# A decoder layer on one core: three seven-product pairs in the second half of the output linear, with sums of weights made beforehand

## The chip, the core and the metric

One Trainium2 core runs one decoder layer in float32. The metric is the time of one execution on the device, in microseconds (us); the median of several runs counts. The engines named here are TensorE (PE in the profile; PEld is its loading of weights), VectorE (DVE), ScalarE (ACT), GpSimd (POOL) and SyncE (SP). SP and POOL issue DMAs, each from a queue that it works off in order.

## What is computed

The layer takes 256 tokens and 16 learned tokens ahead of them (T = 272) of width 2048. It is a SwiGLU feed-forward block, then a mixer of differential attention and a short gated convolution, then a second SwiGLU block and a norm. Cut to what matters here, the reference is:

```python
s = s + 0.5 * swiglu_ffn(rms_norm(s, g1), w_gu1, w_down1)
h = rms_norm(s, g_mix)
q, k, v, b_gate, c_gate, u = jnp.split(h @ w_in, splits, axis=-1)
y_att, y_conv = diff_attention(q, k, v, ...), short_conv_mixer(b_gate, c_gate, u, conv_w)
z = einsum('blnw,nwd->blnd', stack([y_att, y_conv]), w_branch)
merged = sum(sigmoid(h @ w_gate) * z, axis=2)
s = s + merged @ w_out                # the output linear, 2048 x 2048
s = s + 0.5 * swiglu_ffn(rms_norm(s, g2), w_gu2, w_down2)
return rms_norm(s, g_final)[:, 16:]
```

## The kernel before, in words

**Precision.** Each float32 operand is split into a high part and a rest (`parts`, L551 and L552: ScalarE casts the high part, VectorE subtracts for the rest). A product of two blocks is three matmuls: high by high, low by high, high by low (L663 to L665 in `product`). A weight tile is 128 x 1024 (two blocks of 512 columns) or 128 x 512.

**Seven or eight products.** From the gates on, the linears run in `linear_mix`. It takes the 256 tokens as two halves and the columns as two halves of 512, and works through the depth in pairs of 128-row blocks. Each pair is a 2 x 2 by 2 x 2 block product and is one of three kinds:

- **D**: eight products, straight from the loaded weights (two tiles of 1024 columns).
- **S**: seven products in Strassen's manner. VectorE makes the sums of the weights from the loaded blocks just ahead of use (`sums`, L702 to L707), into two tiles t13 and t24.
- **P**: seven products, but t13 and t24 were made early in the kernel and stored in DRAM. The pair loads three blocks of weights (768 KB) and the two tiles (512 KB each, L692 and L693) where D and S load four blocks (1024 KB, L685).

S and P pairs split one tile of 512 columns and three of 1024. They also need sums of the activations: four blocks "sp" per pair, made by `sum_of_parts` on VectorE (L603 to L612), then ScalarE and VectorE (L634, L635). In the output linear those are kept in the pool `aux` (three buffers). A plan at the top of the file gives the kinds of the eight pairs, the positions at which results of an earlier linear are turned, and the tiles behind which `sums` of a later S pair is written. The output linear has two halves of 1024 output columns: `OUT_FIRST` ("DDSDSDSD", S in pairs 2, 4 and 6) and `OUT` ("DDDDSDSD"). `add_mix` (L1210) adds its products to the residual tiles sT. The down linears of the second feed-forward block run three times (thirds of its width) in the same way; the first half of the first two has the plan `DOWN_FIRST`.

**Order of the work.** The framework gives each engine its own order and buffers; the order in the trace is near that of the text but not the same. Weight loads are issued on SP: `load(p + 1)` is written behind the second tile of position p (`far` = 1 in the output linear, 2 in the gate-up linears that load P tiles into `aux`). Loaded weights have three buffers ("st"), split tiles four ("wh", "wl"), and the pool of sums "tt" two. Products are used at most three wide tiles behind their split (`step`, AHEAD = 3). After the last tile of a position one entry of the list `side` is run: transposes, sums and norms that belong to neighbours.

**Sums made early.** `Making` makes half a pair's t13 and t24: POOL fetches the four quarter blocks (L327), VectorE adds three times (L331 to L333), POOL stores (L339). `tick`, called once per 128 rows of the dense linears, spreads these makes over the first feed-forward block (512 ticks). `tick_later` spreads the list `MADE_LATER` over ticks 528 to 636, which are the linears v to u (attention runs beside them); there the makes use the two "tt" buffers. In order of time: first feed-forward block, q, b, then linears k, v, c and u (the ticks' stretch ends at tick 640 with u), gates and branch linears, the output linear's two halves, the second feed-forward block.

Of the kernel before, what the change touches and what calls it, by code (L numbers as in the profile page):

```python
# [9 lines left out]
F32 = mybir.dt.float32  # L10
F32R = mybir.dt.float32r
AF = mybir.ActivationFunctionType
ALU = mybir.AluOpType
# [36 lines left out]
FFN2 = ("DDPPDPPP", (1,), {}, ())  # L50
FFN2_MORE = ("DPPPDSPP", (2,), {(4, 1): 5}, ())
OUT_FIRST = ("DDSDSDSD", (1,), {(1, 1): 2, (3, 1): 4, (5, 1): 6}, ())
OUT = ("DDDDSDSD", (), {(3, 1): 4, (5, 1): 6}, ())
DOWN_FIRST = ("DDDDSDSD", (1,), {(3, 1): 4, (5, 1): 6}, ())
DOWN = ("DDSDSDSD", (), {(1, 1): 2, (3, 1): 4, (5, 1): 6}, ())
DOWN_LAST = ("DDDSDS", (1,), {(2, 1): 3, (4, 1): 5}, ())
# [13 lines left out]
GATE_UNITS = [GATES_FIRST] + [GATES] * (D // GW - 1)  # L70
MADE = [(0, d, p) for d, plan in enumerate(GATE_UNITS) for p, kind in enumerate(plan[0]) if kind == "P"]
MADE += [(1, u, p) for u in range(F // GW) for p, kind in enumerate(_unit_plan(u)[0]) if kind == "P"]
MADE_LATER = [(0, 0, 1), (0, 0, 3), (1, 1, 5), (1, 2, 1), (1, 3, 1)]
MADE = [m for m in MADE if m not in MADE_LATER]
LATER_TICKS = (TICK_COUNT + 16, TICK_COUNT + 124)

# [2 lines left out]
def decoder_layer(ctx: ExitStack, tc: tile.TileContext, t, out):  # L79
# [562 lines left out]
    def linear_mix(plan, a, w, name, done, k0=0, made=None, pairwise=False):  # L642

        kinds, turn_at, sums_at, by_load = plan
        nd = kinds.count("D")
        ns = len(kinds) - nd
        left = {k: 2 * nd * (k in "234x") + ns * (k != "x") for k in "1234567x"}
        ps = {}

        def product(k, left_op, wh, wl):
            first = k not in ps
            if first:
                ps[k] = bank(name + k)  # L660
            left[k] -= 1
            hi, lo = left_op
            nc.tensor.matmul(ps[k], hi, wh, start=first, stop=False)  # L663
            nc.tensor.matmul(ps[k], lo, wh, start=False, stop=False)  # L664
            nc.tensor.matmul(ps[k], hi, wl, start=False, stop=left[k] == 0)  # L665
            if left[k] == 0:
                done(k, ps[k])

        def use(p, n, products):

            for k, left_op, wh, wl in products:
                product(k, left_op, wh, wl)
            if p in turn_at and later:
                later.pop(0)()
            if n == (1 if kinds[p] == "D" else 3):
                if p == 0:
                    flush()
                if side:
                    side.pop(0)()

        def load(p):

            st = wpool.tile([P, 4, GW], F32, tag="st", bufs=ST_BUFS, name="st")
            n = 3 if p in by_load or kinds[p] == "P" else 4
            nc.sync.dma_start(out=st[:, :n, :], in_=w[k0 // 2 + p, :, :n, :])  # L685
            if kinds[p] == "P":
                if pairwise:
                    t13s[p] = wpool.tile([P, 2, GW], F32, tag="tt", bufs=2, name="t13")
                else:
                    t13s[p] = aux.tile([P, 2, GW], F32, tag="act", name="t13")  # L690
                t24s[p] = wpool.tile([P, 2, GW], F32, tag="tt", bufs=2, name="t24")
                nc.sync.dma_start(out=t24s[p], in_=made[p][:, 2:4, :])  # L692
                nc.sync.dma_start(out=t13s[p], in_=made[p][:, 0:2, :])  # L693
            if kinds[p] == "S":
                if not by_load and (made is None or pairwise):
                    t13s[p] = wpool.tile([P, 2, GW], F32, tag="tt", bufs=2, name="t13")
                elif p not in by_load:
                    t13s[p] = aux.tile([P, 2, GW], F32, tag="act", name="t13")
                t24s[p] = wpool.tile([P, 2, GW], F32, tag="tt", bufs=2, name="t24")
            return st  # L700

        def sums(k):  # L702
            st, t13, t24 = loaded[k], t13s[k], t24s[k]
            if k not in by_load:
                nc.vector.tensor_add(t13, st[:, 1:3, :], st[:, 3:4, :].to_broadcast([P, 2, GW]))
            nc.vector.tensor_add(t24[:, 0, :], t13[:, 0, :], st[:, 2, :])
            last_sum[:] = [nc.vector.tensor_add(t24[:, 1, :], t24[:, 0, :], st[:, 0, :]).ins]  # L707

        t13s, t24s = {}, {}

        def prefetch(p):
            t13 = t13s[p] = aux.tile([P, 2, GW], F32, tag="act", name="t13")
            nc.gpsimd.dma_start(out=t13, in_=w[k0 // 2 + p, :, 1:3, :])
            nc.gpsimd.dma_start(out=t13, in_=w[k0 // 2 + p, :, 3:5, :], accum_op=ALU.add)

        far = 2 if by_load or (made is not None and not pairwise) else 1
        loaded = {k: load(k) for k in range(far)}
        for p, kind in enumerate(kinds):
            for k in by_load:
                if k == p + 4 or (p == 0 and k < 4):  # L720
                    prefetch(k)
            st = loaded[p]
            (a11, a21), (a12, a22) = ([a.block(2 * p + c, i) for i in range(2)] for c in range(2))
            if kind == "D":
                tiles = [
                    (st[:, 1 - c :: 2, :], (("2", a1, 0), ("3", a1, 1), ("4", a2, 0), ("x", a2, 1)))
                    for c, (a1, a2) in enumerate(((a11, a21), (a12, a22)))
                ]
            else:
                s1, s2, s3, s4 = a.sums[p]  # L730
                tiles = [
                    (st[:, 2:3, :], (("3", s4, 0),)),
                    (st[:, 0:2, :], (("1", a11, 1), ("2", a12, 0))),
                    (t24s[p], (("6", s2, 0), ("4", a22, 1))),
                    (t13s[p], (("5", s1, 0), ("7", s3, 1))),
                ]
                if kind == "S" and p < len(kinds) - 1:
                    tiles[2:] = tiles[:1:-1]
            for n, (src, products) in enumerate(tiles):
                if n == 1 and p + far < len(kinds):  # L740
                    loaded[p + far] = load(p + far)
                wh, wl = parts(src, src.shape[1])
                if (p, n) in sums_at:

                    with tc.issue_after(part_last[1]):
                        sums(sums_at[p, n])
                products = [(k, left_op, wh[:, j, :], wl[:, j, :]) for k, left_op, j in products]
                step(lambda p=p, n=n, products=products: use(p, n, products), src.shape[1] > 1)
# [458 lines left out]
                out=lo, in0=src, scalar=gain, in1=hi.bitcast(F32), op0=ALU.mult, op1=ALU.subtract  # L1207
            )

    def add_mix(plan, a, w, k0, u, by, adds, end):  # L1210


        v = [[sT[i][u][:, q * GW : (q + 1) * GW] for q in range(2)] for i in range(2)]
# [45 lines left out]
            if all(n in ev for n in "1234567x"):  # L1259
                pending.append(finish_adds)  # L1260

        linear_mix(plan, a, w[u], "pd", done, k0)

    def out_done(u):
        def f():
            if u == 0:
                side.append(lambda: None)
                for p in (0, 2):
                    side.append(lambda p=p: [turned(p), turned(p + 1), squares(0, 0, p // 2), squares(1, 0, p // 2)])
                side.append(lambda: [hn.sum_of_parts(2, tmp), hn.sum_of_parts(3)])  # L1270
            else:
                side.extend(
                    (
                        lambda: [turned(4), squares(0, 1, 0), squares(1, 1, 0)],
                        lambda: [turned(5), hn.sum_of_parts(5)],
                        lambda: [turned(6), squares(0, 1, 1), hn.sum_of_parts(6)],
                        lambda: [turned(7), squares(1, 1, 1)],
                        lambda: hn.sum_of_parts(7),
                        norm_tok,
                    )  # L1280
                )

        return f
# [1 line left out]
    side.extend([lambda: None] * 2)  # L1285
    side.append(lambda: mo.sum_of_parts(6))
    add_mix(OUT_FIRST, mo, w_out, 0, 0, 1.0, "", out_done(0))
    add_mix(OUT, mo, w_out, 0, 1, 1.0, "", out_done(1))

    gfin = [apool.tile([P, W2], F32, tag="act", name=f"gfin{q}") for q in range(2)]  # L1290
    fss = const.tile([P, 2, 2 * 2 + 1], F32, name="fss")
# [32 lines left out]
    for half in thirds:  # L1324
# [14 lines left out]
        for u in range(2):  # L1339
# [32 lines left out]
            if final and u == 0:  # L1372
                side.append(lambda: None)
                side.extend(lambda p=p: ma.sum_of_parts(p) for p in (3, 5))
                add_mix(
                    DOWN_LAST, ma, w_down, half[0] * GC, u, 0.5, "side",
                    lambda score=score: side.extend(
                        lambda iq=iq: [score(*k) for k in iq] for iq in (((0, 0), (1, 0)), ((0, 1),), ((1, 1),))
                    ),
                )  # L1380
            elif u == 0:
                side.extend([lambda: None] * 2)
                side.extend(lambda p=p: ma.sum_of_parts(p) for p in (4, 6, 2))
                add_mix(DOWN_FIRST, ma, w_down, half[0] * GC, u, 0.5, "dma", lambda: None)
            elif not final:
                add_mix(DOWN, ma, w_down, half[0] * GC, u, 0.5, "dma", lambda: None)
            else:
                linear_tok(ops, w_last, chunks, 0, "pd", down, hold=HOLD, side_at=(1, 2, 3, 4, 5))
# [86 lines left out]
```

## Time and profile before

| | |
|---|---|
| median of 3 runs | 2130.33 us |
| the three runs | 2127.54, 2130.33, 2130.54 us |
| the profiled execution, its own time | 2127.0 us |
| its span, first to last instruction | 2125.2 us |
| granted TensorE clock, mean | 0.999 |
| TensorE, VectorE, ScalarE, GpSimd busy | 99%, 84%, 54%, 8% |

A row of a timeline gives start and duration in us, engine, line, operation, output <- input, the number merged, and in brackets the idle time before it with what ended that. Matmuls overlap in the pipeline, so their pace is read from their starts, not from their durations. A row of a group of instructions gives their count, the busy time in us and the mean ns of one. An answer on one tile gives ns as least/median/most.

### The profile page before, as it was taken

What the parts mean: (1) busy time and instruction counts of PE and PEld (TensorE: products, weight loads), DVE (VectorE), ACT (ScalarE), POOL (GpSimd) and SP (SyncE); (2) the same over time, 40 slices, a digit from 0 to 9 for tenths busy, and PEclk for the clock granted to TensorE, in tenths of its full rate; (3) what the DMA queues carried; (4) which work ended last, traced back from release to release, by engine and by line L of the source; (5) the groups of instructions that cost most, each with busy time, mean ns of one, the idle gap of its engine ahead of it and who ended that gap; (6) DMA issues with size and microseconds to landing.
All of it is one profiled execution on the core that took longest, in us unless ns stands there. A gap on an engine that the chain in (4) does not pass through costs nothing.

```text
span 2125.2 us, 33641 instructions
## 1 busy us (share of the span) xinstructions
PE 2114.1 (99%) x13087; PEld 1909.8 (90%) x13087; DVE 1780.5 (84%) x2490; ACT 1151.5 (54%) x1453; POOL 164.8 (8%) x261
## 2 busy tenths in 40 slices
PE   9999999999999999999999999999999999999998
PEld 9999999999999998899998888887888888888887
DVE  8777776677777778978898899989999899998998
ACT  6443343344444445645556555557775567656765
POOL 0111111111111110000000000000000100000000
PEclk9999999999999999999999999999999999999999
DMA  8989999999889885665665665556985988769863
GB/s 307 340 311 338 342 336 333 325 331 331 328 332 336 300 297 192 208 219 201 217 217 195 231 215 196 206 207 243 322 294 198 284 315 305 260 223 316 326 234 139
DMA packets 111329, 576.47 MB, mean 271 GB/s; under 512 B 12993, under 2 KB 13377, under 8 KB 71105
## 3 DMA queue, kind: packets, MB, share of 16 engines
q1 hardware_dynamic: 74160, 444.66, 58.4%
q0 software_dynamic: 36576, 128.99, 17.5%
q8 instruction: 102, 1.67, 0.3%
q10 hardware_dynamic: 432, 0.67, 0.1%
q14 instruction: 59, 0.48, 0.1%
HBM read 506.11 MB, written 63.96 MB: 268 GB/s over the span
## 4 chain that ended last, share of the span: by engine, by line
PE 99%; ACT 1%; DMA 0%; DVE 0%; SPq 0%; issue 0%; ACTq 0%; DVEq 0%
PE pg L663 6%; PE pg L665 6%; PE pg L664 6%; PE pd L447 4%; PE pd L445 4%; PE pu L445 4%; PE pu L446 4%; PE pu L447 4%; PE pd L446 4%; PE pg L445 4%; PE pg L447 4%; PE pg L446 4%; PE pd L663 4%; PE pd L665 4%; PE pd L664 4%; PE g L665 2%
## 5 line engine op out<-in xcount | busy, mean ns | idle before, releaser
L429 ACT CAST wh<-st 128x1024 fp32r<-128x1024 f32 x320 | 335.4, 1049 | 474.1 <-PE pu L446 145.6
L434 DVE TENSOR_TENSOR wl<-st,wh 128x1024 fp32r<-128x1024 f32 x320 | 390.6, 1223 | 212.3 <-ACT wh L429 212.1
L552 DVE TENSOR_TENSOR wl<-st,wh 128x1024 fp32r<-128x1024 f32 (+1 forms) x424 | 453.2, 1085 | 50.2 <-ACT wh L551 45.9
L551 ACT CAST wh<-st 128x1024 fp32r<-128x1024 f32 (+1 forms) x424 | 386.6, 942 | 174.6 <-PE pdx L664 36.9
L551 ACT CAST wh<-t 128x1024 fp32r<-128x1024 f32 x214 | 224.6, 1053 | 205.3 <-DVE t L707 84.0
L552 DVE TENSOR_TENSOR wl<-t,wh 128x1024 fp32r<-128x1024 f32 x214 | 258.1, 1222 | 29.6 <-ACT wh L551 25.0
L447 PE MATMUL pd<-mh,wl 128*128 128x272 f32 x704 | 203.1, 288 | 0.0
L445 PE MATMUL pd<-mh,wh 128*128 128x272 f32 x704 | 202.2, 287 | 0.0
L445 PE MATMUL pg<-h,wh 128*128 128x272 f32 x704 | 201.9, 287 | 0.1
L445 PE MATMUL pu<-h,wh 128*128 128x272 f32 x704 | 201.9, 287 | 0.0
L446 PE MATMUL pg<-h,wh 128*128 128x272 f32 x704 | 201.7, 287 | 0.0
L447 PE MATMUL pu<-h,wl 128*128 128x272 f32 x704 | 201.7, 287 | 0.0
L446 PE MATMUL pu<-h,wh 128*128 128x272 f32 x704 | 201.7, 286 | 0.0
L447 PE MATMUL pg<-h,wl 128*128 128x272 f32 x704 | 200.9, 287 | 0.0
L446 PE MATMUL pd<-ml,wh 128*128 128x272 f32 x704 | 200.7, 285 | 0.0
L664 PE MATMUL pg<-wh,h 128*128 128x512 f32 x375 | 146.7, 391 | 0.0
L663 PE MATMUL pg<-wh,h 128*128 128x512 f32 x375 | 146.3, 390 | 0.0
L665 PE MATMUL pg<-wl,h 128*128 128x512 f32 x375 | 145.5, 389 | 0.0
L339 POOL DMA_DIRECT2D made<-mk x118 | 86.3, 731 | 756.4 <-DVE mk L333 607.0
L446 PEld LDWEIGHTS pd<-ml,wh 128*128 128x128 f32 x704 | 133.4, 190 | 0.0
L445 PEld LDWEIGHTS pg<-h,wh 128*128 128x128 f32 x704 | 132.9, 189 | 0.3 <-ACT wh L429 0.3
L446 PEld LDWEIGHTS pg<-h,wh 128*128 128x128 f32 x704 | 132.7, 189 | 0.1
(392 smaller groups left out, 5101.8 us busy)
## 6 DMA issues: line engine op xcount, KB each, us to landing
st<-in_ffn_w_gu_dram SPq DMA_DIRECT2D x118, 1024.0 KB, 7.3
st<-in_ffn_w_down_dram SPq DMA_DIRECT2D x82, 1024.0 KB, 7.2
mk<-in_ffn_made_of_dram POOLq DMA_DIRECT2D x118, 512.0 KB, 8.6
made<-mk POOLq DMA_DIRECT2D x118, 512.0 KB, 6.5
t<-made SPq DMA_DIRECT2D x118, 512.0 KB, 6.1
st<-in_ffn_w_gu_dram SPq DMA_DIRECT2D x54, 768.0 KB, 6.0
st<-in_w_in_dram SPq DMA_DIRECT2D x32, 1024.0 KB, 5.2
st<-in_w_gate_dram SPq DMA_DIRECT2D x27, 1024.0 KB, 4.8
```

Source lines behind the costliest of these rows:

```text
L339: last_store[:] = [nc.gpsimd.dma_start(out=self.unit[self.p][:, :, cs], in_=self.t).ins]
L429: nc.scalar.copy(out=wh[:, :m, :], in_=sw)
L434: last_wl[:] = [nc.vector.tensor_sub(wl[:, :m, :], sw, wh[:, :m, :].bitcast(F32)).ins]
L445: nc.tensor.matmul(a, wh[:, i, f], act.part(c, 0, t0, t1), start=first, stop=False)
L446: nc.tensor.matmul(a, wh[:, i, f], act.part(c, 1, t0, t1), start=False, stop=False)
L447: nc.tensor.matmul(a, wl[:, i, f], act.part(c, 0, t0, t1), start=False, stop=last)
L551: part_last[:] = [nc.scalar.copy(out=wh, in_=src).ins]
L552: part_last.append(nc.vector.tensor_sub(wl, src, wh.bitcast(F32)).ins)
L663: nc.tensor.matmul(ps[k], hi, wh, start=first, stop=False)
L664: nc.tensor.matmul(ps[k], lo, wh, start=False, stop=False)
L665: nc.tensor.matmul(ps[k], hi, wl, start=False, stop=left[k] == 0)
```

## The change

The second half of the output linear gets the plan `DDDPDPPD` and the order of pairs 0 1 3 2 5 4 6 7; its P pairs are pairs 2, 4 and 6, in positions 3, 5 and 6. Their sums of weights join `MADE_LATER`, whose makes grow from ten to sixteen in the same 108 ticks. The last field of a plan, which listed pairs whose first sums a DMA would add and was empty in every plan, now is the order of pairs; the code behind it goes. In `DOWN_FIRST`'s `side` list, the sum of parts of pair 2 comes one entry later.

```diff
-OUT = ("DDDDSDSD", (), {(3, 1): 4, (5, 1): 6}, ())
+OUT = ("DDDPDPPD", (), {}, (0, 1, 3, 2, 5, 4, 6, 7))
...
-MADE_LATER = [(0, 0, 1), (0, 0, 3), (1, 1, 5), (1, 2, 1), (1, 3, 1)]
+MADE_LATER = [(0, 0, 1), (0, 0, 3), (2, 1, 2), (2, 1, 4), (2, 1, 6), (1, 1, 5), (1, 2, 1), (1, 3, 1)]
...
-        kinds, turn_at, sums_at, by_load = plan
+        kinds, turn_at, sums_at, pairs = plan
+        pairs = pairs or tuple(range(len(kinds)))
...
-            n = 3 if p in by_load or kinds[p] == "P" else 4
-            nc.sync.dma_start(out=st[:, :n, :], in_=w[k0 // 2 + p, :, :n, :])
+            n = 3 if kinds[p] == "P" else 4
+            nc.sync.dma_start(out=st[:, :n, :], in_=w[k0 // 2 + pairs[p], :, :n, :])
...
-                nc.sync.dma_start(out=t24s[p], in_=made[p][:, 2:4, :])
-                nc.sync.dma_start(out=t13s[p], in_=made[p][:, 0:2, :])
+                nc.sync.dma_start(out=t24s[p], in_=made[pairs[p]][:, 2:4, :])
+                nc.sync.dma_start(out=t13s[p], in_=made[pairs[p]][:, 0:2, :])
...
-        far = 2 if by_load or (made is not None and not pairwise) else 1
+        far = 2 if made is not None and not pairwise else 1
...
-            (a11, a21), (a12, a22) = ([a.block(2 * p + c, i) for i in range(2)] for c in range(2))
+            (a11, a21), (a12, a22) = ([a.block(2 * pairs[p] + c, i) for i in range(2)] for c in range(2))
...
-                s1, s2, s3, s4 = a.sums[p]
+                s1, s2, s3, s4 = a.sums[pairs[p]]
...
-    def add_mix(plan, a, w, k0, u, by, adds, end):
+    def add_mix(plan, a, w, k0, u, by, adds, end, made=None):
...
-        linear_mix(plan, a, w[u], "pd", done, k0)
+        linear_mix(plan, a, w[u], "pd", done, k0, made, True)
...
-    add_mix(OUT, mo, w_out, 0, 1, 1.0, "", out_done(1))
+    add_mix(OUT, mo, w_out, 0, 1, 1.0, "", out_done(1), made[2][1])
...
-                side.extend(lambda p=p: ma.sum_of_parts(p) for p in (4, 6, 2))
+                side.extend(lambda p=p: ma.sum_of_parts(p) for p in (4, 6))
+                side.extend((lambda: None, lambda ma=ma: ma.sum_of_parts(2)))
```

## Rows read from the trace of the kernel before

**Rows 1.** The page: busy time, then the chain that ended last by engine.
```profile
PE 2114.1 (99%) x13087; PEld 1909.8 (90%) x13087; DVE 1780.5 (84%) x2490; ACT 1151.5 (54%) x1453; POOL 164.8 (8%) x261
...
PE 99%; ACT 1%; DMA 0%; DVE 0%; SPq 0%; issue 0%; ACTq 0%; DVEq 0%
```

**Rows 2.** Stretches: PE, PEld, DVE, ACT, POOL busy us, then clock, DMA, GB/s.
```profile
1388.00:1432.00 44.00, 43.83 (x202) 36.14 (x201) 39.41 (x57) 26.16 (x38) 0.00 (x0) 1.00 0.57 199
...
1480.00:1600.00 120.00, 120.00 (x542) 98.74 (x541) 115.47 (x134) 87.13 (x105) 0.00 (x0) 1.00 0.86 302
```

**Rows 3.** TensorE's timeline, output linear's second half: first and last of 42.
```profile
1389.98 0.39 PE L663 MATMUL pd<-wh,mg 128*128 128x512 f32 x1
...
1399.27 0.39 PE L665 MATMUL pdx<-wl,mg 128*128 128x512 f32 x1
```

**Rows 4.** The same timeline, start of position 6.
```profile
1422.60 0.39 PE L664 MATMUL pd<-wh,mg 128*128 128x512 f32 x1
1423.16 0.50 PE L663 MATMUL pd<-wh,sp 128*128 128x512 f32 x1 [0.17 <-ACT wh L551]
1423.50 0.40 PE L664 MATMUL pd<-wh,sp 128*128 128x512 f32 x1
```

**Rows 5.** ScalarE's timeline just ahead of rows 4.
```profile
1421.02 1.06 ACT L551 CAST wh<-t 128x1024 fp32r<-128x1024 f32 x1 [1.96 <-DVE t L707]
1421.98 0.62 ACT L634 CAST sp<-sums 128x512 fp32r<-128x512 f32 x1
1422.49 1.57 ACT L551 CAST wh<-st 128x512 fp32r<-128x512 f32 x2
```

**Rows 6.** Groups of VectorE by line and shape, 1386 to 1433 us.
```profile
L552 DVE TENSOR_TENSOR wl<-st,wh 128x1024 fp32r<-128x1024 f32 x15 | 18.2, 1219 | 3.1 <-ACT wh L551 1.5 <-PE h_ps L1201 1.4
...
L705 DVE TENSOR_TENSOR t<-st 128x1024 f32<-128x1024 f32 x2 | 2.4, 1217 | 0.0
...
L706 DVE TENSOR_TENSOR t<-t,st 128x512 f32<-128x512 f32 x2 | 1.4, 684 | 0.0
```

**Rows 7.** TensorE's timeline, first half of the first down linear, position 6.
```profile
1633.57 0.39 PE L664 MATMUL pd<-wh,m 128*128 128x512 f32 x1
1634.07 0.50 PE L663 MATMUL pd<-wh,sp 128*128 128x512 f32 x1
```

**Rows 8.** The tile of the makes, mk, from 780 to 1080 us.
```profile
L332 DVE TENSOR_TENSOR mk<-mk x11: 411/424/426, 783.1 to 1064.4; 128x256 f32<-128x256 f32 x11
L333 DVE TENSOR_TENSOR mk<-mk x11: 404/424/426, 783.5 to 1064.9; 128x256 f32<-128x256 f32 x11
...
L331 DVE TENSOR_TENSOR mk<-mk x10: 630/684/689, 907.3 to 1063.7; 128x512 f32<-128x512 f32 x10
...
  PEld po L1007: 0.4, 1
...
DMA to landing us min/median/max: 3.1/5.8/7.5
```

**Rows 9.** Stretches in linears v to u, columns as rows 2; then their sum.
```profile
1030.00:1055.00 25.00, 25.00 (x210) 24.51 (x209) 24.01 (x53) 12.67 (x22) 1.27 (x2) 1.00 0.55 178
...
sum 175.00, PE 175.00 PEld 166.91 DVE 142.81 ACT 88.53 POOL 12.07; mean PE 25.00 PEld 23.84 DVE 20.40 ACT 12.65 POOL 1.72
```

**Rows 10.** Timelines of POOL, SP and PE: last store, first gate load, first gate matmul.
```profile
1065.71 0.71 POOL L339 DMA_DIRECT2D made<-mk  x1 [9.16 <-DVE rsao L285]
...
1072.85 0.38 SPq L685 DMA_DIRECT2D st<-in_w_gate_dram  x1
...
1090.96 0.39 PE L663 MATMUL g<-wh,h 128*128 128x512 f32 x1
```

**Rows 11.** Landing: tiles t of all 118 P loads; then 1 MB of w_out.
```profile
DMA to landing us min/median/max: 3.7/6.1/10.2
...
DMA to landing us min/median/max: 4.6/4.9/5.9
```

**Rows 12.** Waits of TensorE over the whole span: us in total, times, longest.
```profile
PE h_ps L1201 <- DVE sT L1217: 0.9, 2, 0.6
```

More of the change, by code (lines that the diff above doesn't have):

```diff
@@ L691, in load @@
                 t24s[p] = wpool.tile([P, 2, GW], F32, tag="tt", bufs=2, name="t24")
-                nc.sync.dma_start(out=t24s[p], in_=made[p][:, 2:4, :])
-                nc.sync.dma_start(out=t13s[p], in_=made[p][:, 0:2, :])
+                nc.sync.dma_start(out=t24s[p], in_=made[pairs[p]][:, 2:4, :])
+                nc.sync.dma_start(out=t13s[p], in_=made[pairs[p]][:, 0:2, :])
             if kinds[p] == "S":
-                if not by_load and (made is None or pairwise):
+                if made is None or pairwise:
                     t13s[p] = wpool.tile([P, 2, GW], F32, tag="tt", bufs=2, name="t13")
-                elif p not in by_load:
+                else:
                     t13s[p] = aux.tile([P, 2, GW], F32, tag="act", name="t13")
@@ L703, in sums @@
             st, t13, t24 = loaded[k], t13s[k], t24s[k]
-            if k not in by_load:
-                nc.vector.tensor_add(t13, st[:, 1:3, :], st[:, 3:4, :].to_broadcast([P, 2, GW]))
+            nc.vector.tensor_add(t13, st[:, 1:3, :], st[:, 3:4, :].to_broadcast([P, 2, GW]))
             nc.vector.tensor_add(t24[:, 0, :], t13[:, 0, :], st[:, 2, :])
@@ L709, in linear_mix @@
         t13s, t24s = {}, {}
[L711 to L714, printed above, removed]
-        far = 2 if by_load or (made is not None and not pairwise) else 1
+        far = 2 if made is not None and not pairwise else 1
         loaded = {k: load(k) for k in range(far)}
         for p, kind in enumerate(kinds):
-            for k in by_load:
-                if k == p + 4 or (p == 0 and k < 4):
-                    prefetch(k)
             st = loaded[p]
-            (a11, a21), (a12, a22) = ([a.block(2 * p + c, i) for i in range(2)] for c in range(2))
+            (a11, a21), (a12, a22) = ([a.block(2 * pairs[p] + c, i) for i in range(2)] for c in range(2))
             if kind == "D":
```

## The prediction, made before the run

> **What bounds the kernel now.** I read the page first, then the busy time by stretches, then TensorE's timeline around the edit, then what the other engines and the DMA queues do there. The page shows TensorE busy 99% of the span, and the chain that ended last is TensorE at 99% [rows 1]. A busy share alone proves little, so the stretch of the edited half (1388 to 1432 us) was looked at by starts: 42 matmuls of 512 columns start without a hole from 1389.98 to 1399.27, which is 9.29 / 41 = 0.227 us each [rows 2, 3]. Three matmuls make a product, so a product costs 0.68 us and nothing but TensorE's own pace sets the time there. VectorE is the second limit, with 39.41 of 44 us [rows 2]. A gain can come only from matmuls that go away and from the few holes between them.
>
> One such hole lies in the edited half: the matmul that follows 1422.60 starts at 1423.16, 0.33 us late, and the next is late by 0.34 - 0.23 = 0.11, together 0.44 us [rows 4]. The reader is to see its cause on ScalarE: it stood idle 1.96 us until L707, the last sum of weights of an "S" pair, then cast that sum, then a tile of the norm's sums, and only then came to the tile for which TensorE waited [rows 5].
>
> **Part 1, the products.** Before, the half had six D pairs (8 products) and two S pairs (7): 62 products. After, it has five D and three P: 61. One product of three matmuls goes: **-0.68 us**, on the path.
>
> **Part 2, the sums on VectorE.** Two S pairs made their sums here: 2 x (1.22 + 0.68 + 0.68) = 5.2 us of VectorE [rows 6]. They go. The pair that turns from D to P splits four tiles instead of two, one more of 1024 columns (1.22 us) and one of half that size: about +1.9 us. Net, VectorE has 3.3 us less in 44. It has no hole to give back but the 0.44 us, because ScalarE no longer stands behind L707: **-0.44 us**. Bounds: 0 if another wait takes its place, -0.44 if not; I take the second, since the row names the removed instruction as the cause.
>
> **Part 3, the loads of the P pairs.** Each P pair loads 768 KB plus two 512 KB tiles where 1 MB came before. The two tiles share two buffers (tt), so those of pair 6, in position 6, wait until position 5 has split its own. These waits stand in SP's in-order queue, and behind them are position 7's load and the loads of the next linear. By a clock that starts when TensorE ends position 3, with 0.68 us a product: position 4 ends at 5.44, position 5 at 10.20, and position 6 needs its two tiles at 12.24 and 13.60. A tile is cast once TensorE has released the buffer four tiles back, so the splits in position 5 begin at 0 and 2.72; cast 1.06 and subtraction 1.22 take 2.28 [rows 5, 6]. The transfers thus start at 2.3 and 5.0. Such a tile lands after 3.7 to 10.2 us, at the median 6.1 [rows 11]: at 8.4 and 11.1. The first also waits for its cast's buffer until 8.84. With 2.28 for the split they are ready at 11.1 and 13.4, against 12.24 and 13.60: hidden, but the second by only 0.2 us. Position 7's 1 MB starts at about 5.4, lands by 5.9 later at most [rows 11], is split from 11.3 and needed at 14.96: hidden. At a landing of 10.2 the second tile is ready at 17.5, 3.9 us late. So the price is **0**, with ends 0 and +3.9; I take the median because it comes from the same kind of transfer in a busier stretch. Position 5's own tiles reuse those of position 3, with the D pair of position 4 (5.44 us) between them, and have that much more room. A gain is excluded, since nothing here waits for a load now.
>
> **Part 4, the sums made early.** Three pairs in two halves are six more makes: per make a fetch and a store on POOL's queue, which is idle nearly all the time here, and three adds on VectorE, 0.68 + 0.42 + 0.42 = 1.53 us [rows 8]. That is 6 x 1.53 = 9.2 us of VectorE, in linears where it is busy 142.8 of 175 us [rows 9]. Eleven steps in 108 ticks become 17, one in 6.4 instead of 9.8 ticks. Over some 170 us that is 10 us a step; a transfer of a make lands within 7.5 [rows 8], so an add need not wait for its fetch. Cover: the 32 us that VectorE idles. If the cover failed, all 9.2 would show; if it holds, 0. One row shows what a make costs now: one TensorE weight load waited 0.4 us for a make's add, in ten makes [rows 8]. Six more at that rate: **+0.24 us**, which I take, being nearest to it. A gain is excluded: this only adds.
>
> The last store moves from tick 627 to 630 of 640. It is at 1065.71 and the linear ends at 1090.96, so a tick is at most 25.3 / 13 = 1.9 us and the store moves by at most 5.8. SP's tile load behind it and the first gate load (1072.85) move with it, to 1078.7; that load lands by 5.9 later, is split by 1087, and TensorE needs it at 1090.96 [rows 10]. Hidden by 4 us.
>
> **Part 5, the first half of the down linear, twice.** The sum of parts of pair 2 moves one step later. Here the same hole as in part 2 stands ahead of position 6: 0.50 - 0.23 = 0.27 us at 1634.07 [rows 7], and by the pattern of [rows 4] about 0.11 in the matmul behind it, so 0.38; the linear runs twice, and the second time the trace has the same hole. With the sum gone from ahead of L707 the cast comes earlier: **-0.76 us** for both. Ends: -0.76, and 0 if the moved sum (an add of 512 columns, four of 128 and a split) makes the same hole one position later. I take the first, since VectorE's work up to the next pair's split is the same in total.
>
> Edits with one answer: the new order of pairs and the dropped prefetch branch change no count; the sums of pairs 2, 4 and 6 were made for the first half already.
>
> **Sum.** -0.68 - 0.44 - 0.76 + 0.24 = -1.64 us against the profiled execution's 2127.0 us, so 2125.4. That execution lies 3.3 us under the median of 2130.33; the three runs spread by 3.0. On the median the same step gives 2130.33 - 1.64 = **2128.7 us**, -0.08%. A measurement of this kernel can tell about 0.2%, 4.3 us, from no change; this is less.
>
> **Rivals.**
> - VectorE becomes the bound from linear v to u (slower). From 1030 to 1055 us it is busy 24.01 of 25 [rows 9]; an even share of the added 9.2 us is 1.4, more than the 1.0 left. It decides once the delay outgrows the split tiles held ahead. Against it: 32 us idle in the whole stretch, and no long wait of TensorE there. Fully shown: -1.88 + 9.2 = +7.3, 2137.7 us. Chance 0.07.
> - SP's queue binds at position 6 (part 3): 2128.7 + 3.9 = 2132.6, still within 0.2%. For: only 0.2 us of room at the median. Against: the landing of 10.2 is the slowest of 118. Chance 0.11.
> - The three transfers of a P pair run one after another. By rows, the 768 KB at no less than a 512 KB tile's 3.7 us and two tiles at 3.7 make 11.1 us a pair; three of them and two loads of 4.9 are 43 us, where TensorE has 25.2 for positions 3 to 7. Even with a D pair's lead of 5.4 that adds 12 us: 2141. Against it: from 1480 to 1600 us, P pairs run back to back at 302 GB/s with TensorE busy 120.00 of 120 [rows 2], so transfers overlap. Chance 0.02. The Trainium skill ("DMA: Bandwidth & Descriptors", section "Anatomy of one DMA — SWDGE (gpsimd) path") gives every DMA a fixed 2 us beside its bytes and so speaks against cutting a load in three; by it the pair's transfers, if each waited for the one before, would take about 10 us. No row shows such waiting: the fastest tile's 3.7 us [rows 11] stands beside the page's 3.2 for its size, but the rate of 1480 to 1600 us [rows 2] is that of transfers that overlap.
> - The edit moves the holes and doesn't close them: the instructions in the trace are not in the order of the text, and a new order can put another cast ahead. Then -0.68 + 0.24, 2129.9. Chance 0.07.
> - Faster by over 0.2%: with 0.9 us of waits of the next linear's transposes for VectorE [rows 12] also gone, I reach only -2.8; what is left is the spread between sets of runs. Chance 0.04.
>
> **How the numbers follow.** The forecast has 0.69. Same: 0.69 + 0.11 + 0.07 = 0.87; slower 0.07 + 0.02 = 0.09; faster 0.04. The range takes the spread of the runs and the bounds: from 2127.5 less 2.8, about 2124.5, to 2130.5 plus 3.9 less 1.6, 2133. The two slower rivals lie outside it.
>
> **What would show it.** Right: 369 matmuls of the output linear become 366, no hole ahead of position 6, none at the down linears' position 6, and TensorE's waits from linear v to u as before. Wrong: SP's tile loads in position 6 landing after TensorE's need, a hole of a microsecond or more there; ScalarE waiting for tiles in positions 5 to 7; VectorE without idle time from 1005 to 1080 us with TensorE waiting for its splits; or a difference of over 4 us either way.

## The result, and the profile after

The kernel became slower: 2136.77 us in the median of 6 runs (2136.41 to 2137.82) against 2128.51 for 6 runs of the kernel before (2127.54 to 2130.54). The ratio is **1.0041 [1.0031, 1.0051]**, so 8.3 us are lost. The forecast was 2128.7 with a range up to 2133.0, and a chance of 0.87 for no change: it was wrong, in the sign and in the range.

The profiled execution after took 2137.27 us (span 2135.5), that of before 2127.0 (span 2125.2): 10.3 us apart. Of this, 8.3 is the difference of the medians; the execution of before lies 1.5 under its median of six, that of after 0.5 over its own.

The page after, engines busy, answers to [rows 1]:

```profile
PE 2117.4 (99%) x13084; PEld 1913.2 (90%) x13084; DVE 1785.1 (84%) x2504; ACT 1151.5 (54%) x1455; POOL 172.1 (8%) x273
```

Three matmuls fewer, as the diff says, and still a TensorE that is busy 3.3 us longer at 99%. The shares show nothing of the loss. So I cut both traces at four events that any version has: the first matmul of linear v, the last one of the branch linears (z), the last one of the first third's gate-up linears (pg), and the end.

| stretch, us | before | after | difference |
|---|---|---|---|
| start to v (code that the edit doesn't touch) | 899.0 | 900.0 | +1.0 |
| v to last z | 446.95 | 454.81 | **+7.86** |
| last z to last pg (output linear, gate-up units 0 to 3) | 254.23 | 256.08 | **+1.85** |
| of that, output linear, first to last pd | 86.64 | 86.44 | -0.20 |
| last pg to end (down linears and the rest) | 525.02 | 524.61 | -0.41 |

The first row is spread: over all twelve profiles of this case it goes from 898.9 to 901.3. In after it holds a wait of 1.47 us for weights of the first linear, 9 us from the start, which before doesn't have. The other stretches repeat more closely and carry the comparisons below.

The waits of TensorE over the whole span (us in all, times, longest). The rows left out between these lie in the first 15 us. The kernel before has none of the three below:

```profile
PE aT L984 <- DVE scM L975: 4.1, 2, 2.1
PE pg L664 <- ACT wh L551: 2.1, 1, 2.1
...
PE pd L666 <- DVE wl L552: 0.5, 1, 0.5
```

They are the three places: attention beside linears k and u, the border between gate-up units 0 and 1, and position 6 of the edited half. All that TensorE waited for in the kernel before from 785 to 1345 us (linear q to the branch linears) is this:

```profile
PE qb_ps L897 <- ACT u2x L757: 0.2, 1, 0.2
```

**Place 1: linears v to u.** The first `aT` hole on TensorE's timeline:

```profile
942.15 0.29 PE L446 MATMUL k<-h,wh 128*128 128x272 f32 x1
944.50 0.45 PE L984 MATMUL aT<-ident,sc 128*128 128x128 f32 x1 [2.06 <-DVE scM L975]
...
944.97 0.43 PE L445 MATMUL k<-h,wh 128*128 128x272 f32 x1
945.20 0.43 PE L446 MATMUL k<-h,wh 128*128 128x272 f32 x1
```

TensorE stands idle for 2.06 us until VectorE's L975, the end of a softmax of attention. After it, matmuls of the linear start 0.23 us apart; ahead of it they start 0.12 to 0.13 apart. The stretches say why (PE, PEld, DVE, ACT and POOL busy, then the granted clock):

```profile
944.50:947.70 3.20, 3.20 (x15) 3.20 (x16) 2.40 (x4) 1.58 (x3) 0.00 (x0) 0.50 0.39 119
948.00:951.00 3.00, 3.00 (x25) 2.71 (x25) 2.25 (x7) 1.39 (x3) 0.00 (x0) 1.00 0.71 298
```

For 3.2 us the granted clock was 0.50, the lower level (1.2 GHz), so 1.6 us more went. One hole costs 2.1 + 1.6, or about 3.7 us. The second one is like it:

```profile
1036.68 0.66 PE L984 MATMUL aT<-ident,sc 128*128 128x128 f32 x2 [2.07 <-DVE scM L975]
...
1036.70:1039.90 3.20, 3.20 (x15) 3.20 (x16) 2.56 (x6) 0.54 (x2) 1.26 (x2) 0.50 0.40 116
```

Two make 7.4 of the 7.86. The Trainium skill ("TensorE: Matmul & The Clock Gate", section "HAM oscillation — how this bites in real kernels") describes waits for a DMA that put the array back to its lower clock. The trace agrees that the clock falls behind a wait, 0.50 behind 2.06 us of idle time, though this wait is for VectorE and the waits of its example are longer (3 to 5 us).

Why was L975 late? VectorE's timeline ahead of it:

```profile
933.91 1.23 DVE L434 TENSOR_TENSOR wl<-st,wh 128x1024 fp32r<-128x1024 f32 x1 [2.36 <-ACT wh L429]
938.35 0.69 DVE L331 TENSOR_TENSOR mk<-mk 128x512 f32<-128x512 f32 x1 [3.22 <-DMA mk<-in_ffn_made_of_dram]
...
944.27 0.23 DVE L975 SCALAR_TENSOR_TENSOR scM<-sc,rs 128x16 f32<-128x16 f32 x1
```

VectorE was free at 935.14 and stood for 3.22 us at a make's first add, whose fetch had not landed. Everything of the softmax was queued behind that add. That VectorE is strictly first in, first out, the Trainium skill says too ("Perfetto Trace Analysis", section "Tensor Engine Instruction (MATMUL, LD_WEIGHTS)"); the trace agrees, with 3.22 us of idle time ahead of L331. POOL's timeline shows the fetch (L327) and the store (L339):

```profile
930.23 0.71 POOL L339 DMA_DIRECT2D made<-mk  x1 [9.28 <-DVE mk L333]
930.88 0.61 POOL L327 DMA_DIRECT2D mk<-in_ffn_made_of_dram  x1
940.38 0.71 POOL L339 DMA_DIRECT2D made<-mk  x1 [8.89 <-DVE sc L960]
941.02 0.62 POOL L327 DMA_DIRECT2D mk<-in_ffn_made_of_dram  x1
```

The fetch went out at 930.88 and was needed at 935.14, 4.3 us later; it landed after 7.4. Store to fetch 0.65, fetch to add 7.47, adds 1.6, and 0.4 to the store make 10.1 us: the chain of one make is as long as the step of 10 us that the prediction reckoned with. The steps in the trace are uneven (from fetch to fetch 8.3 to 16.2 us, 11.9 in the mean), and those around this hole are 9.8, 10.5 and 10.1, with nothing to spare. Of VectorE's waits from 890 to 1100 us, 11.5 us are of this kind, in four waits:

```profile
DVE mk L331 <- DMA mk<-in_ffn_made_of_dram: 11.5, 4, 3.2
```

In each of the four VectorE came to the add 3.9 to 4.8 us behind the fetch. In the kernel before, where the steps were 11.0 to 26.5 us, it never came earlier than 7.8 us behind it, no fetch landed later than 7.5, and there is no such wait. Only two of the four waits let TensorE run dry; the first and the last (2.5 us ahead of 917.6 and 3.0 ahead of 1072.1) left no hole in it.

**Place 2: position 6.** It answers to [rows 4, 5]. SP's timeline, the load of pair 6's first sum tile:

```profile
1423.74 0.33 SPq L693 DMA_DIRECT2D t<-made  x1
```

ScalarE's timeline, the cast of that tile:

```profile
1430.79 1.05 ACT L551 CAST wh<-t 128x1024 fp32r<-128x1024 f32 x1 [0.76 <-DMA t<-made]
```

TensorE's timeline behind it:

```profile
1432.30 0.40 PE L665 MATMUL pd<-wh,sp 128*128 128x512 f32 x1
1433.15 0.50 PE L666 MATMUL pd<-wl,sp 128*128 128x512 f32 x1 [0.45 <-DVE wl L552]
```

The old hole behind L707 is gone. In its place the tile lands 6.9 us after its issue, and ScalarE waits for it. By the starts of the matmuls less their pace, the hole is 0.85 - 0.23 = 0.62, with 0.11 in the next matmul 0.73 us.

**Place 3: gate-up units 0 and 1.** Nothing of the edit is here, and no step of the prediction. TensorE's timeline:

```profile
1490.19 0.39 PE L666 MATMUL pgx<-wl,h 128*128 128x512 f32 x1
1492.69 0.50 PE L664 MATMUL pg<-wh,h 128*128 128x512 f32 x1 [2.11 <-ACT wh L551]
```

And ScalarE's, the cast that released it:

```profile
1491.59 2.00 ACT L551 CAST wh<-st 128x1024 fp32r<-128x1024 f32 x2 [5.33 <-DMA st<-in_ffn_w_gu_dram]
```

Unit 1's first weights came too late for TensorE, and after 2.11 us of idle time the granted clock of the next 4.3 us was 0.63:

```profile
1492.70:1497.00 4.30, 4.30 (x12) 3.32 (x13) 4.30 (x5) 4.00 (x6) 0.00 (x0) 0.63 0.20 58
```

Counted from the last z, TensorE began unit 0's last matmul at 135.4 us, where it was 137.5 before. So 2.1 us had been gained by then; the hole (2.3 by the starts) and the clock (1.6) turned that into +1.85 us.

**The down linears** came out as forecast. The same place as [rows 7], without a hole:

```profile
1633.64 0.39 PE L666 MATMUL pdx<-wl,m 128*128 128x512 f32 x1
1633.87 0.39 PE L664 MATMUL pd<-wh,sp 128*128 128x512 f32 x1
1634.10 0.39 PE L665 MATMUL pd<-wh,sp 128*128 128x512 f32 x1
```

### The profile page after: what moved, and what is told of

Read it like the earlier page. It is cut to its first block, busy times and chain, and to the rows that moved or that the text cites. A ratio compares the mean times of both kernels' runs of the same rounds, so it can differ in the third digit from the quotient of the medians.

```text
span 2135.5 us, 33699 instructions
## 1 busy us (share of the span) xinstructions
PE 2117.4 (99%) x13084; PEld 1913.2 (90%) x13084; DVE 1785.1 (84%) x2504; ACT 1151.5 (54%) x1455; POOL 172.1 (8%) x273
## 4 chain that ended last, share of the span: by engine, by line
PE 52%; DVE 1%; DMA 1%; ACT 1%; issue 0%; POOL 0%; ACTq 0%; DVEq 0%
PE pg L666 6%; PE pg L664 6%; PE pg L665 6%; PE pd L666 3%; PE pd L664 3%; PE pd L665 3%; PE g L665 2%; PE g L664 2%; PE g L666 2%; PE z L479 1%; PE z L481 1%; PE z L480 1%; PE pdx L664 1%; PE pdx L666 1%; PE pdx L665 1%; DMA mk<-in_ffn_made_of_dram 1%
## 5 line engine op out<-in xcount | busy, mean ns | idle before, releaser
L339 POOL DMA_DIRECT2D made<-mk x124 | 90.3, 729 | 769.7 <-DVE mk L333 662.3
```

The lines of the kernel that those rows point to most:

```text
L339: last_store[:] = [nc.gpsimd.dma_start(out=self.unit[self.p][:, :, cs], in_=self.t).ins]
```

## The experiments

The theory: the loss from v to u comes from the distance of fetch and add, not from VectorE's work; the one from z to pg comes from late transfers. The main rival is the one on record, VectorE as the bound. "Before" of each ratio is a fresh set of runs beside it.

**One part at a time.** The first kernel makes the six sums and never reads them; its plan and its down linears are those of before.

```diff
-OUT = ("DDDPDPPD", (), {}, (0, 1, 3, 2, 5, 4, 6, 7))
+OUT = ("DDDDSDSD", (), {(3, 1): 4, (5, 1): 6}, ())
...
-    add_mix(OUT, mo, w_out, 0, 1, 1.0, "", out_done(1), made[2][1])
+    add_mix(OUT, mo, w_out, 0, 1, 1.0, "", out_done(1))
...
-                side.extend(lambda p=p: ma.sum_of_parts(p) for p in (4, 6))
-                side.extend((lambda: None, lambda ma=ma: ma.sum_of_parts(2)))
+                side.extend(lambda p=p: ma.sum_of_parts(p) for p in (4, 6, 2))
```

> The kernel before with the six more makes in the same ticks, which nothing reads; the output linear and the down linears are those of before. Theory (a make's first add waits on VectorE for its fetch, attention and then TensorE wait behind it): two holes of about 2 us at TensorE's turns of the attention scores, each with some us at the lower clock behind it, and nothing after the linear u: about +8 us against the kernel before (it was +7.9 at the first gate matmul in the changed kernel's profile, the start's +1.0 not counted). Rival (the cost comes from the P pairs' loads): no change, within 1 us.

Measured: 2138.88 us, ratio 1.0051 [1.0038, 1.0065]. From v to z 455.26 us, +8.31; from z to pg 253.51, -0.72. Its long waits of TensorE from 785 to 1345 us:

```profile
PE aT L984 <- DVE scM L975: 4.0, 2, 2.0
```

and those of VectorE for makes from 890 to 1100:

```profile
DVE mk L331 <- DMA mk<-in_ffn_made_of_dram: 12.3, 5, 3.2
```

The makes alone bring the whole loss. The second kernel has the P pairs and no new makes; its P pairs read the sums that were made for gate-up unit 5, and the down linears are as before.

```diff
-MADE_LATER = [(0, 0, 1), (0, 0, 3), (2, 1, 2), (2, 1, 4), (2, 1, 6), (1, 1, 5), (1, 2, 1), (1, 3, 1)]
+MADE_LATER = [(0, 0, 1), (0, 0, 3), (1, 1, 5), (1, 2, 1), (1, 3, 1)]
...
-    add_mix(OUT, mo, w_out, 0, 1, 1.0, "", out_done(1), made[2][1])
+    add_mix(OUT, mo, w_out, 0, 1, 1.0, "", out_done(1), {2: made[1][5][1], 4: made[1][5][2], 6: made[1][5][3]})
```

> The changed kernel with the ten makes of before and the old order of sums in the down linears; the three P pairs read the tiles made for gate-up unit 5 (wrong numbers in the output linear's second half, the same loads and matmuls). Theory: the output linear and the opening of the second feed-forward block gain 1.4 us as in the changed kernel, and the hole of 2.3 us between gate-up units 0 and 1 with its 1 us of lower clock stays, since it comes from the order of the loads: about +2 us against before. Rival (that hole comes from the makes' delay upstream): -1.4 us.

Measured: 2127.18 us, ratio 0.9996 [0.9987, 1.0004]. From v to z -0.16 us, from z to pg -0.29. Position 6 has a hole of 0.19 + 0.11, and the border of units 0 and 1 one of 1.74. The theory's +2 us did not come: the hole stayed, as it said, but full clock followed it. The third kernel is before with the later sum of parts in the down linears, and nothing else:

```diff
-                side.extend(lambda p=p: ma.sum_of_parts(p) for p in (4, 6, 2))
+                side.extend(lambda p=p: ma.sum_of_parts(p) for p in (4, 6))
+                side.extend((lambda: None, lambda ma=ma: ma.sum_of_parts(2)))
```

> The kernel before with the sum of parts of pair 2 one step later in the two down linears and nothing else. Theory: the holes of 0.38 us at position 6 close, -0.8 us. Rival (the sum makes the hole one position later): 0. Either lies under what the times can tell; the two holes in the trace decide.

Measured: 2126.58 us, ratio 0.9994 [0.9985, 1.0003]. From pg to the end 524.28 against 525.02: **-0.74**, and no hole is left in the two linears. The stretch shows the gain; the ratio can't tell it from nothing.

**The fetch two steps ahead.** The change with all its makes, adds and transfers; only each fetch is written a step earlier (it then waits for the store ahead of it, which uses the same buffer):

```diff
-        if i < len(spare_later):
-            with tc.issue_after(last_store[0]):
-                spare_later[i].fetch(N_AUX + i % 2, i < 2)
+        for j in (0, 1) if not i else (i + 1,):
+            if j < len(spare_later):
+                with tc.issue_after(last_store[0]):
+                    spare_later[j].fetch(N_AUX + j % 2, j < 2)
```

> The changed kernel with each of the late makes fetched two steps ahead of its adds, not one, in the same two buffers (the fetch waits on POOL's queue for the store before it to land). The same adds, transfers and matmuls. Theory (the adds wait for fetches): the two holes from linear k to u close, about -7.5 us against the changed kernel, 2129 us. Rival (the 9.2 us of added VectorE work themselves are the price): no change against the changed kernel, 2137 us.

Measured: 2127.39 us, ratio 0.9999 [0.9990, 1.0008]. From v to z 447.66: +0.71 in place of +7.86. VectorE's wait for `mk` is gone, and this is all that TensorE waits for from 785 to 1345 us:

```profile
PE qb_ps L890 <- ACT u2x L750: 0.2, 1, 0.2
```

In the same 175 us as [rows 9] VectorE is busy here for (its busy time, and its instructions, in the row that sums seven stretches):

```profile
sum 175.00, DVE 148.65; mean DVE 21.24
```

That is 5.8 more than before's 142.81, and TensorE waits for none of it. After the change, VectorE was busy less around the first hole than before, since it stood waiting. Its busy time there, after, then before:

```profile
930.00:955.00 25.00, 16.66 (x38) 0.93 0.64 217
...
930.00:955.00 25.00, 18.77 (x45) 1.00 0.69 250
```

So VectorE's work is not the bound; its order with a DMA ahead of it is. A last version of the makes puts them into the first block instead, where `tick` already fetches ahead:

```diff
-MADE_LATER = [(0, 0, 1), (0, 0, 3), (2, 1, 2), (2, 1, 4), (2, 1, 6), (1, 1, 5), (1, 2, 1), (1, 3, 1)]
-MADE = [m for m in MADE if m not in MADE_LATER]
+MADE_LATER = [(0, 0, 1), (0, 0, 3), (1, 1, 5), (1, 2, 1), (1, 3, 1)]
+MADE = [m for m in MADE if m not in MADE_LATER] + [(2, 1, 2), (2, 1, 4), (2, 1, 6)]
```

> The changed kernel with the six makes of the output linear's pairs in the first feed-forward block (114 there instead of 108, in 512 ticks, each fetched three steps ahead), and the ten late makes as before. Theory (a make costs nothing where its fetch has time): linears k to u as in the kernel before, no hole there, the first feed-forward block within 0.5 us of before, in all about 2127 us. Rival (DMA is busy 90% there and VectorE waits for fetches): the first block longer by 2 us or more.

Measured: 2126.79 us, ratio 0.9994 [0.9985, 1.0003]. The first block doesn't grow (start to v 898.9), v to z is 447.57. Two different cures, the same 7 us. Most of the 0.6 us that are left here is the same wait once more: the last fetch of the ten late makes landed after 10.1 us, VectorE waited 2.3 us for it, and TensorE 0.5 us for VectorE in linear u.

**The hole between units 0 and 1.** With the fetch ahead, the hole is still there, 1.36 us. (Holes of this border are given by starts here; the idle time in a row's brackets is 0.16 less.) The three first gate-up loads of unit 1 on SP's timeline, before:

```profile
1477.52 0.33 SPq L685 DMA_DIRECT2D st<-in_ffn_w_gu_dram  x1
...
1478.66 0.33 SPq L685 DMA_DIRECT2D st<-in_ffn_w_gu_dram  x1
...
1480.58 0.33 SPq L685 DMA_DIRECT2D st<-in_ffn_w_gu_dram  x1
```

and the landing of the loads issued by that line from 1470 to 1490 us:

```profile
DMA to landing us min/median/max: 4.8/5.3/6.4
```

The same two views after, first SP's timeline:

```profile
1483.55 0.33 SPq L686 DMA_DIRECT2D st<-in_ffn_w_gu_dram  x1
...
1485.28 0.33 SPq L686 DMA_DIRECT2D st<-in_ffn_w_gu_dram  x1
...
1485.88 0.85 SPq L686 DMA_DIRECT2D st<-in_ffn_w_gu_dram  x1
```

then the landing:

```profile
DMA to landing us min/median/max: 7.6/8.0/9.3
```

Three loads in 3.1 us land in 5 to 6.4, three in 2.3 us in 8 to 9.3. In after the first of them went out 2.8 us earlier than before, counted from the last z, and landed no earlier: at 136.7 us, against 136.6. That is 0.95 us ahead of unit 0's last matmul before, and 1.33 behind it after. The pattern parts the runs: 2.3 us in after and in the kernels with the plan of the change or a plain alternation, with holes of 1.4 to 2.3; 3.1 us in before, in the first and third experiment and in the two below that alternate and end in two D pairs, with holes of 0 to 0.8. The two tile loads ahead of the three are part of the pattern: all five go out within 6.0 us in the one, within 7.9 to 8.2 in the other, so no run says which of them counts. Which pattern comes follows the order of work ahead of it, so the next kernel changes that order alone. P pairs alternate with D pairs, and two D pairs stand last:

```diff
-OUT = ("DDDPDPPD", (), {}, (0, 1, 3, 2, 5, 4, 6, 7))
+OUT = ("DPDPDPDD", (), {}, (0, 2, 1, 4, 3, 6, 5, 7))
```

> The run with the fetches two steps ahead, and P and D pairs alternating in the output linear's second half: DPDPDPDD with pairs 0 2 1 4 3 6 5 7. Theory (the hole of 0.7 us in position 6 is the wait of pair 6's tiles for the two buffers of pair 4's): with a D pair between all P pairs it closes, so the two halves of the output linear take 0.7 us less than with the fetches ahead alone (86.5 us there), near 85.7; what it gains arrives at the hole between gate-up units 0 and 1 and may be lost there. Rival (VectorE's backlog makes that hole): it moves to another position and the halves still take about 86.4 us. The time within 1.5 us of the kernel before either way.

Measured, with the fetch ahead: **2125.37 us, ratio 0.9987 [0.9978, 0.9996]**. No hole at position 6 and none at the border; from z to pg 251.93, -2.30 us. TensorE's waits of the whole execution:

```profile
PE pg L446 <- ACT wh L430: 1.4, 1, 1.4
PE warm L105 <- DVE ones L99: 1.1, 1, 1.1
PE pg L665 <- ACT sp L635: 0.2, 1, 0.2
PE qb_ps L890 <- ACT u2x L750: 0.2, 1, 0.2
```

Both long ones lie in the first 15 us. The 85.7 us that were expected for the two halves read 86.7 from first to last pd; five matmuls of the next linear (1.1 us) stand ahead of the last pd here. The time fell by more than the 1.5 us expected, since the hole at the border went too. Is it the alternation or the two D pairs at the end? A plain alternation that ends P, D:

```diff
-OUT = ("DDDPDPPD", (), {}, (0, 1, 3, 2, 5, 4, 6, 7))
+OUT = ("DDPDPDPD", (), {}, ())
```

> The run with the fetches two steps ahead, with the pairs in their natural order and P and D alternating, DDPDPDPD. Theory (two P pairs one behind the other make the hole in position 6 and bunch the loads that follow): no hole over 0.3 us in positions 2 to 7, no hole over 0.5 us between gate-up units 0 and 1, about 2125.5 us as in the alternating run. Rival (it matters that the last P pair ends two positions before the end, so that its tiles are free for the next linear's): the hole between the units stays over 1 us, about 2127 us.

Measured, with the fetch ahead: 2130.10 us, ratio 1.0008 [0.9999, 1.0016]; from z to pg 257.07, +2.84. The theory was wrong here: alternating is not enough. TensorE, where the last P pair of the half meets the next linear:

```profile
1434.70 0.40 PE L666 MATMUL pg<-wh,h 128*128 128x512 f32 x1
1436.19 0.50 PE L665 MATMUL pd<-wh,sp 128*128 128x512 f32 x1 [1.09 <-ACT wh L552]
```

Products of the last P pair (`pd`) now stand behind products of the next linear (`pg`) and wait, and a hole of 1.93 us stands at the border. The granted clock fell behind the hole at the border, too:

```profile
1486.38 0.50 PE L665 MATMUL pg<-wh,h 128*128 128x512 f32 x1 [1.78 <-ACT wh L552]
...
1488.00:1490.00 2.00, 2.00 (x6) 1.58 (x5) 2.00 (x4) 2.00 (x3) 0.00 (x0) 0.50 0.02 6
```

The place of the last P pair counts.

Two kernels with the fetch ahead disturb what lies just ahead of unit 1's loads. The first makes one sum of parts less for the gate-up linears (pair 7 reads pair 6's); the second adds a 512 KB store on POOL's queue:

```diff
-                        lambda: hn.sum_of_parts(7),
+                        lambda: hn.sums.__setitem__(7, hn.sums[6]),
```

> The run with the fetches two steps ahead, without the sum of activations of pair 7 for the second feed-forward block (pair 6's is used in its place, so the gate-up products of pair 7 are wrong): about 2 us of VectorE and 0.6 us of ScalarE less in gate-up unit 0, the same transfers and matmuls. Theory A (VectorE, busy over 95% there, sets when the load buffers come free, and so the hole between units 0 and 1): the hole of 1.36 us closes or falls under 0.5 us. Theory B (the transfers themselves, five of them within 6 us, land late): the hole stays between 1 and 2 us.

```diff
+            self.sp = sp
...
-                        lambda: hn.sum_of_parts(7),
+                        lambda: [
+                            hn.sum_of_parts(7),
+                            nc.gpsimd.dma_start(out=kept.tile([P, 4, 2, P], F32R, name="extra"), in_=hn.sp),
+                        ],
```

> The run with the fetches two steps ahead, and one more store of 512 KB, issued from POOL when the sum of activations of pair 7 is ready, near 1475 us, which nothing reads. Theory A (VectorE sets the hole between gate-up units 0 and 1): the hole stays between 1 and 2 us. Theory B (the DMA engines are shared by too many transfers there): it grows by about 512 KB / 330 GB/s = 1.6 us, to 2.5 us or more.

Measured: without the sum 2125.78 us, ratio 0.9989 [0.9980, 0.9998], and the hole is gone, but SP also issues the loads in another order, the first at 1471.34, so the run doesn't say which of the two did it: VectorE's work there remains a possible cause. With the store 2128.37 us, 1.0001 [0.9992, 1.0010]; the store went out at 1474.24 and landed after 5.9, beside the loads, which landed after 7.4, 7.6 and 8.8 against 7.0, 7.2 and 8.4. The hole grew from 1.36 to 1.63 only. More bytes in flight at that time are a small part of it.

**The best of both.** Makes in the first block, and the alternating order with two D pairs last (the two diffs above):

> The six makes in the first feed-forward block and the late ten as before, as in the run named made early, with the output linear's second half in the alternating order DPDPDPDD of the run named alternate. Theory (the two repairs act in different stretches and add up): linears v to u within 0.7 us of before, no hole at position 6 nor between gate-up units 0 and 1, the median between 2124 and 2126 us, and a clear 0.1% under the kernel before. Rival (the hole between the units comes back with any other upstream timing): a hole of over 1 us there, and 2127 us.

Measured: **2125.25 us, ratio 0.9986 [0.9977, 0.9995]**. From v to z +0.09, from z to pg -1.82, the rest -0.47: -2.2 us, beside -3.0 of the medians (2128.2 for before). It and the version with the fetch ahead in the same order are the two kernels with nothing left out that beat both, by 0.13 to 0.14% against before; between the two no run tells.

## Why the prediction was wrong

- **Part 4 is the step that failed**, in the words "10 us a step; a transfer of a make lands within 7.5, so an add need not wait for its fetch". The numbers came near: the landing ahead of the first hole was 7.4 us, the slowest of the sixteen 7.6, the mean step 11.9. The conclusion failed, for two reasons. An average step was compared with a landing, but what counts is when VectorE, in its own order, gets to the add: 4.3 us after the fetch, where it was 7.8 or more before. And the step has to hold the whole chain of store, fetch, landing and adds, 10.1 us by the rows, not the landing alone; the steps are uneven, and the four waits fall into steps of 9.6 to 10.7 us. The "cover" of 32 idle us was there, too, and of no use, since idle time of an engine can't be spent on what stands behind a waiting instruction. The price of an added wait is read from what is queued behind it; the prediction did this for SP's queue and not for VectorE's.
- **Its price** was set at 0.24 with ends 0 and 9.2. The measured 7.86 lies inside these ends by chance: 9.2 was the adds' own time, the loss is two holes and the lower clock behind them. Where the wait is taken away by the earlier fetch, the same makes cost 0.7 in that stretch (five kernels), not 0.24; no single wait shows where.
- **The end of part 4** was off, too, at no cost. The last store was to move by 5.8 us at most; counted from the first matmul of v it moved by 19.8 (by 10.8 with the fetch ahead), and TensorE's first gate matmul waited for nothing.
- **The first rival** (VectorE the bound from v to u, 2137.7 us, chance 0.07) named the place and, nearly, the time, but not the mechanism: VectorE was less busy around the hole than before, and its 148.65 of 175 us made TensorE wait nowhere when the fetch was ahead.
- **Part 1** held: 3 matmuls fewer. **Part 2** held in its cause (the hole behind L707 is gone) and not in its sum, for **part 3** put another hole in the same place: 0.73 us in after and 0.69 with the fetch ahead, where 0 was taken and 3.9 was the end. The clock of part 3 was near: transfers started 3.2 and 5.1 us after its zero (2.3 and 5.0 forecast), landing 6.9 and 6.4 (6.1 taken). With 0.2 us of room by its own working, the price should have been some tenths. The rival of SP's queue came true in small. The output linear gained 0.20 us, where -0.68 - 0.44 was forecast and -0.68 - 0.44 + 0.73 = -0.39 would follow. Most of the 0.2 between them are two more starts that come 0.31 us behind the one before in place of 0.23 (four such before, six after).
- **The rival of transfers one after another** (12 us more) was not seen: the half lost 0.73 us to a load.
- **Part 5** held: -0.76 forecast, -0.74 with that edit alone, -0.38 to -0.58 in the kernels with the other edits beside it.
- **Not in the prediction at all** is the hole between units 0 and 1, some 50 us behind the edit. It took back the 2.1 us that TensorE was ahead there, and 1.85 more. The prediction followed the queues up to the first loads of the next linear only.

What stays open: why three loads take 8 to 9.3 us in one rhythm and 5 to 6.4 in the other. The rhythm goes with the holes in every version that issues these loads in this order, but the kernel that was to separate its cause changed the order of loads as well, and 0.5 MB more in flight explains 0.3 us.

## What to carry to other kernels

An instruction that waits for a DMA on an in-order engine charges its wait to all that is queued behind it, and TensorE pays when it needs some of that before the wait is made good (two of four times here): compare the landing with the time from the fetch to the moment that engine reaches the instruction, and fetch a step further ahead before adding such work. Count a hole of TensorE with what follows at the lower clock. When work is taken out of one linear, look at the first loads of the next two for what the earlier arrival meets.

## What the runs showed of the hardware

- Two holes of 2.06 and 2.07 us were followed by a granted clock of 0.50 (1.2 GHz) for some 3 us, one of 2.11 by 0.63 over 4.3 us. One of 1.78 us, in the kernel with the plain alternation, was followed by 0.79 over 1.6 us and 0.50 over the next 2; one of 1.58 us, in the second experiment, by full clock:

```profile
1484.10:1488.00 3.90, 3.90 (x17) 3.05 (x18) 3.90 (x5) 3.90 (x6) 0.00 (x0) 1.00 0.23 91
```

- The first of unit 1's loads landed after 4.9 to 5.7 us in the five kernels in which the third followed 3.1 us behind it, and after 7.0 to 8.0 in the six with 2.3 us. TensorE's hole was 0 to 0.8 us in the ones, 1.4 to 2.3 in the others.
- Sums added by VectorE during the first block (six more makes, 9.2 us of its time by [rows 8]) cost nothing that shows there: 898.9 us to linear v against 899.0.
